# Last block before each normalisation: the second token half's product as two products of 256 columns

## The chip, the core and the metric

The kernel runs on one core of one Trainium2 chip. The metric is the device time of one execution in microseconds. Every profile shown is of one execution, taken by the hardware profiler.

## The reference

A trunk of two decoder layers over 256 tokens of width 2048, float32. Each layer is a token mixer and a gated ConvFFN (inner width 5632), and each sub-layer ends in a residual sum and a LayerNorm:

```python
for layer in range(DEPTH):
    if layer % N_MIXERS == 0:
        mixed = hgrn2_mixer(h, hg_w_in[occ], hg_norm_g[occ], hg_w_out[occ], lower_bounds[layer])
    else:
        mixed = chunked_gmlp(h, sg_w_in[occ], ..., sg_w_out[occ])
    h = layer_norm(ALPHA * h + mixed, ln1_g[layer], ln1_b[layer])
    ffn = conv_ffn(h, ffn_w_up[layer], ...)
    h = layer_norm(ALPHA * h + ffn, ln2_g[layer], ln2_b[layer])
```

`layer_norm` needs the mean and the variance of a whole row of 2048 values before any of it can be scaled. There are four such norms, one behind each sub-layer.

## The kernel before

**Data.** The 256 tokens are two halves of 128, `t` = 0 and 1. `z` (128 x 2 x 2048) holds the residual stream by tokens. `X` and `Y` hold activations turned, feature on the partition, as a rounded part `hi` and a rest `lo`; a product is three matmuls (hi by hi, hi by lo, lo by hi). Weights come as chunks of 4 x 128 rows by 512 columns (`CK`, `NB`): one DMA on the SP queue into `raw` (`fetch`, L80, 3 buffers), a cast to `whi` on ScalarE (L97) and a subtraction to `wlo` on VectorE (L98), each in two pieces. There are 3 buffers of `whi` and `wlo`, and one extra in the pool `xp`, so that four chunks can be held at a joint. `chunk` takes the next chunk and keeps three on the way (`ahead`).

**Products.** `block_a` makes tokens by features: for each column block of 512 it accumulates over the chunks into one PSUM tile for each token half (L127 to L129), then calls `evac`. With `staggered`, which is set for the last column block (`c == 3`) before a norm, the chunks are held and half 0 is finished and evacuated before half 1 begins (L144 to L149). `block_b` makes features by tokens (L163, L170); with `halves`, in the first FFN block behind a norm, all products that need only half 0 of the tokens come before those that need half 1 (L183 to L186). The first block of the gMLP input does the same with three chunks in `block_a`. The HGRN output uses `staggered_pass` (L664 to L679): one chunk for each of the four column blocks, half 0 through all four, then half 1.

**Joint.** `add_z` gives the evacuation: VectorE adds PSUM into `z` (L398, L400) and, in the last pass, takes `bn_stats` over the 512 columns (L402); after block 3 of a token half `after` runs: `bn_aggr` (L335), a square root on ScalarE (L336), a reciprocal (L337), four rescales of `z` (L371), and `turn`: four times four transposes on TensorE (L308) into a PSUM tile `pt` (2 buffers), scale and bias by three ScalarE activations (L315) and one VectorE row (L317) into `turn` (2 buffers), then a cast into `X` on ScalarE and a subtraction into `X` on VectorE (both L320). Behind the last norm two VectorE rows apply scale and bias (L365, L368) and `z` is stored. `tc.high_priority()` wraps these evacuations. A scheduler sets the order of rows on each engine when the program is built; on the chip each engine runs its rows in that order.

The norms stand behind `hgrn_out` (joint 1), `ffn(0)` (joint 2), `gmlp` (joint 3) and `ffn(1)` (the end).

Of the kernel before, what the change touches and what calls it, by code (L numbers as in the profile page):

```python
# [8 lines left out]
F32 = mybir.dt.float32  # L9
# [6 lines left out]
P = 128  # L16
# [7 lines left out]
LN_EPS = 1e-5  # L24
RMS_EPS = 1e-6
NB = 512
CK = 4
HEADS = 16
LEVELS = (1, 4, 16)
# [11 lines left out]
class Trunk:  # L41
# [72 lines left out]
    def block_a(self, act, ka, w, k0, nch, c0, evac, staggered=False, halves=False):  # L114

        nc = self.nc
        ps = [self.acc.tile([P, NB], F32, tag="acc", name="pa") for _ in range(2)]
        n = [0, 0]

        def part(ch, ci, t):  # L120
            hi, lo = ch
            for kk in range(CK):
                k = ka + ci * CK + kk
                xh = act[:, k, 0, t * P : (t + 1) * P]
                xl = act[:, k, 1, t * P : (t + 1) * P]
                last = n[t] == nch * CK - 1
                nc.tensor.matmul(ps[t], xh, hi[:, kk, :], start=n[t] == 0, stop=False)  # L127
                nc.tensor.matmul(ps[t], xh, lo[:, kk, :], start=False, stop=False)  # L128
                nc.tensor.matmul(ps[t], xl, hi[:, kk, :], start=False, stop=last)  # L129
                n[t] += 1  # L130

        take = lambda ci: self.chunk(w, k0 + ci * CK, c0)
        first = max(0, nch - 4) if staggered else nch
        head = []
        if halves:
            head = [take(ci) for ci in range(min(3, nch))]
            for t in range(2):
                for ci, ch in enumerate(head):
                    part(ch, ci, t)
        for ci in range(len(head), first):  # L140
            ch = take(ci)
            for t in range(2):
                part(ch, ci, t)
        held = [take(ci) for ci in range(first, nch)]  # L144
        for t in range(2):
            for i, ch in enumerate(held):
                part(ch, first + i, t)
            if held:
                evac(t, ps[t])  # L149
        if not held:  # L150
            for t in range(2):
                evac(t, ps[t])

    def block_b(self, act, w, nch, c0, evac, halves=False):

# [184 lines left out]
    def norm(self, name, l, store=None):  # L340


        nc = self.nc
        g, b = self.a[name + "_g"][l], self.a[name + "_b"][l]
        self.ln = ExitStack()
        self.lnp = self.ln.enter_context(
            self.tc.tile_pool(name=f"{name}{l}", bufs=1, side="right")
        )
        self.xps = ExitStack()
        self.xp = self.xps.enter_context(  # L350
            self.tc.tile_pool(name=f"x{name}{l}", bufs=1, side="right")
        )
        self.stats = [
            self.small.tile([P, 4, 6], F32, tag=f"stats{t}", name="stats") for t in range(2)
        ]
        self.gbc = [self.broadcast(self.lnp, g, c, f"g{c}") for c in range(4)]
        self.bbc = [self.broadcast(self.lnp, b, c, f"b{c}") for c in range(4)]

        def after(t):
            mv = self.mean_rstd(self.stats[t])  # L360
            mean, rstd = mv[:, 0:1], mv[:, 1:2]
            for c in range(4):
                zz = self.z[:, t, c * NB : (c + 1) * NB]
                if store:
                    nc.vector.scalar_tensor_tensor(  # L365
                        zz, zz, mean, self.gbc[c], ALU.subtract, ALU.mult
                    )
                    nc.vector.scalar_tensor_tensor(zz, zz, rstd, self.bbc[c], ALU.mult, ALU.add)  # L368
                    store(t, c)
                else:  # L370
                    nc.vector.tensor_scalar(zz, zz, mean, rstd, ALU.subtract, ALU.mult)  # L371
                    self.turn(t, 4 * c, g=(name + "_g", l), b=(name + "_b", l))

        self.after_stats = after
# [11 lines left out]
    def add_z(self, c, first=False, last=False):  # L386


        nc = self.nc

        def evac(t, ps):
            with self.tc.high_priority() if last else nullcontext():
                step(t, ps)

        def step(t, ps):
            zz = self.z[:, t, c * NB : (c + 1) * NB]
            if first:
                nc.vector.scalar_tensor_tensor(zz, zz, ALPHA, ps, ALU.mult, ALU.add)  # L398
            else:
                nc.vector.tensor_tensor(zz, zz, ps, ALU.add)  # L400
            if last:
                nc.vector.bn_stats(self.stats[t][:, c, :], zz)  # L402
                if c == 3:
                    self.after_stats(t)

        return evac
# [257 lines left out]
    def staggered_pass(self, act, ka, w, k0):  # L664

        nc = self.nc
        ev = [self.add_z(c, last=True) for c in range(4)]
        held = [self.chunk(w, k0, c * NB) for c in range(4)]
        for t in range(2):
            for c in range(4):  # L670
                hi, lo = held[c]
                ps = self.acc.tile([P, NB], F32, tag="acc", name="pa")
                for kk in range(CK):
# [229 lines left out]
```

## Time and profile before

| | |
|---|---|
| median of 3 runs | 2241.09 us (2240.43 to 2241.46) |
| the profiled execution's own time | 2240.33 us |
| its span | 2238.6 us |
| TensorE busy | 2216.0 us, 99% |
| VectorE busy | 1470.8 us, 66% |
| ScalarE busy | 1106.0 us, 49% |
| DMA | 430.14 MB, 192 GB/s on average |

Shares are over the whole span. In the stretch around a joint they differ: from 1505 to 1515 us TensorE is busy for 8.84 of 10 us and VectorE for all 10. Times in rows are from the start of the span. A row of the timeline gives start, duration, engine, line and shape, and in brackets the idle time ahead of it with what ended it. A row's duration reaches past the start of the next row on the same engine where they are pipelined, so the time a row takes of its queue is read from start to start.

### The profile page before, as it was taken

The page shows a single profiled execution, that of the slowest core. Times are in us where ns is not written, and L with a number is a line of the kernel's source. Part 1 is how long each engine was busy: PE and PEld are TensorE (multiplying, and loading weights), DVE is VectorE, ACT ScalarE, POOL GpSimd, SP SyncE. Part 2 cuts the span into 40 slices and gives each one's busy share as a digit, 9 for nine tenths or more (in the row PEclk, how much of TensorE's full clock was granted, in tenths as well). Part 3 has the DMA queues.
Part 4 walks back from the last instruction along what each step waited for, and adds up shares of the span by engine and source line. Part 5 has one row for each costly group of instructions (what it writes and reads, how often), then busy time and mean ns, then how long its engine had stood idle before and what let it go on. Part 6 is the DMA issues. An engine that isn't in the chain of part 4 may idle for free.

```text
span 2238.6 us, 31751 instructions
## 1 busy us (share of the span) xinstructions
PE 2216.0 (99%) x12781; PEld 1910.7 (85%) x12781; DVE 1470.8 (66%) x2327; ACT 1106.0 (49%) x1698; POOL 48.4 (2%) x102
## 2 busy tenths in 40 slices
PE   8999999999999999999999999999999999999998
PEld 7888888889888888888888888888888888888886
DVE  5877677667675666456666676566765666466755
ACT  5666565646443554344444545455544444344542
POOL 4000000000000000000000000000000000000000
PEclk9999999999999999999999999999999999999999
DMA  7454645555566555555555675655565655555563
GB/s 262 157 180 144 204 151 170 207 169 191 204 222 197 198 192 189 197 198 188 191 199 177 211 224 185 231 182 188 188 230 184 207 189 196 198 188 191 185 207 113
DMA packets 214052, 430.14 MB, mean 192 GB/s; under 512 B 7544, under 2 KB 8336, under 8 KB 213904
## 3 DMA queue, kind: packets, MB, share of 16 engines
q1 hardware_dynamic: 209536, 415.26, 55.5%
q0 software_dynamic: 4368, 12.85, 1.9%
q8 instruction: 100, 1.64, 0.3%
q14 instruction: 48, 0.39, 0.0%
HBM read 425.98 MB, written 2.10 MB: 191 GB/s over the span
## 4 chain that ended last, share of the span: by engine, by line
PE 94%; DVE 2%; ACT 1%; issue 1%; DMA 1%; SPq 0%; POOL 0%; DVEq 0%; POOLq 0%; ACTq 0%
PE pb L163 37%; PE pb L170 19%; PE pa L128 12%; PE pa L129 12%; PE pa L127 12%; DVE wlo L98 1%; PE pl L553 1%; PE pt L308 1%; ACT whi L97 1%; PE pg L755 0%; DMA bb<-in_sg_ln_b_dram 0%; PE pa L676 0%; PE pa L677 0%; PE pa L678 0%; DMA z<-in_x_dram 0%
## 5 line engine op out<-in xcount | busy, mean ns | idle before, releaser
L98 DVE TENSOR_TENSOR wlo<-raw,whi 128x1024 fp32r<-128x1024 f32 (+1 forms) x786 | 930.3, 1218 | 660.4 <-ACT whi L97 652.1
L163 PE MATMUL pb<-X,whi 128*128 128x512 f32 (+1 forms) x3960 | 1302.6, 384 | 1.9 <-DVE X L320 1.9
L97 ACT CAST whi<-raw 128x1024 fp32r<-128x1024 f32 (+1 forms) x786 | 790.1, 1047 | 859.3 <-PE pb L163 396.0
L170 PE MATMUL pb<-X,wlo 128*128 128x256 f32 x3840 | 1037.4, 278 | 0.0
L163 PEld LDWEIGHTS pb<-X,whi 128*128 128x128 f32 x3960 | 725.2, 188 | 143.5 <-DVE X L320 2.4
L170 PEld LDWEIGHTS pb<-X,wlo 128*128 128x128 f32 x3840 | 713.4, 188 | 5.9
L128 PE MATMUL pa<-wlo,Y 128*128 128x512 f32 x928 | 361.5, 390 | 0.0
L127 PE MATMUL pa<-whi,Y 128*128 128x512 f32 x928 | 361.4, 389 | 0.0
L129 PE MATMUL pa<-whi,Y 128*128 128x512 f32 x928 | 361.3, 389 | 0.0
L127 PEld LDWEIGHTS pa<-whi,Y 128*128 128x128 f32 x928 | 174.3, 188 | 36.0
L128 PEld LDWEIGHTS pa<-wlo,Y 128*128 128x128 f32 x928 | 174.3, 188 | 35.9
L129 PEld LDWEIGHTS pa<-whi,Y 128*128 128x128 f32 x928 | 174.3, 188 | 35.7
L208 ACT COPY rest<-pb 128x256 f32<-128x256 f32 x240 | 87.6, 368 | 100.9 <-PE pb L163 96.4
L128 PE MATMUL pa<-wlo,X 128*128 128x512 f32 x256 | 99.9, 390 | 0.0
L127 PE MATMUL pa<-whi,X 128*128 128x512 f32 x256 | 99.8, 390 | 0.0
L129 PE MATMUL pa<-whi,X 128*128 128x512 f32 x256 | 99.7, 389 | 0.0
L808 DVE SCALAR_TENSOR_TENSOR act<-a,cols,act 128x254 f32<-128x254 f32 (+1 forms) x176 | 73.1, 478 | 0.0
L128 PEld LDWEIGHTS pa<-wlo,X 128*128 128x128 f32 x256 | 48.1, 188 | 9.9
L129 PEld LDWEIGHTS pa<-whi,X 128*128 128x128 f32 x256 | 48.1, 188 | 9.8
L127 PEld LDWEIGHTS pa<-whi,X 128*128 128x128 f32 x256 | 48.1, 188 | 9.8
L400 DVE TENSOR_TENSOR z<-z,pa 128x512 f32<-128x512 f32 x40 | 27.3, 684 | 32.9 <-PE pa L129 29.0
L812 ACT ACTIVATE act<-act 128x256 f32<-128x256 f32 x88 | 33.8, 415 | 12.0 <-DVE act L808 11.8
(164 smaller groups left out, 1029.5 us busy)
## 6 DMA issues: line engine op xcount, KB each, us to landing
raw<-in_ffn_w_up_dram SPq DMA_DIRECT2D x176, 1024.0 KB, 4.9
raw<-in_ffn_w_down_dram SPq DMA_DIRECT2D x88, 1024.0 KB, 4.9
raw<-in_hg_w_in_dram SPq DMA_DIRECT2D x63, 1024.0 KB, 5.2
raw<-in_sg_w_in_dram SPq DMA_DIRECT2D x32, 1024.0 KB, 5.4
raw<-in_hg_w_out_dram SPq DMA_DIRECT2D x16, 1024.0 KB, 5.1
raw<-in_sg_w_out_dram SPq DMA_DIRECT2D x16, 1024.0 KB, 4.9
g<-in_ln_g_dram POOLq DMA_DIRECT2D x16, 256.0 KB, 6.4
b<-in_ln_b_dram POOLq DMA_DIRECT2D x16, 256.0 KB, 9.2
```

Of the source, the lines that this page charges most:

```text
L97: nc.scalar.copy(hi[:, s, :], raw[:, s, :])
L98: self.last_lo = nc.vector.tensor_tensor(lo[:, s, :], raw[:, s, :], hi[:, s, :].bitcast(F32), ALU.subtract)
L127: nc.tensor.matmul(ps[t], xh, hi[:, kk, :], start=n[t] == 0, stop=False)
L128: nc.tensor.matmul(ps[t], xh, lo[:, kk, :], start=False, stop=False)
L129: nc.tensor.matmul(ps[t], xl, hi[:, kk, :], start=False, stop=last)
L163: nc.tensor.matmul(ps[j][:, :, s], ch[0][:, k % CK, c], act[:, k, :, s], start=start and k == 0, stop=k == last, skip_group_check=halves,)
L170: nc.tensor.matmul(ps[j][:, 1, :], ch[1][:, k % CK, c], act[:, k, 0, :], start=False, stop=False, skip_group_check=halves,)
L208: nc.scalar.copy(r, ps[:, 1, :])
L308: nc.tensor.transpose(ps[:, j, :], self.z[:, t, k * P : (k + 1) * P], self.ident)
L400: nc.vector.tensor_tensor(zz, zz, ps, ALU.add)
L808: nc.vector.scalar_tensor_tensor(cv[:, d:], x[:, : S - d], self.c(("cw", l, 2 - d), f), cv[:, d:], ALU.mult, ALU.add,)
L812: nc.scalar.activation(cv, cv, AF.Silu)
```

## The change

In the last column block before each norm, half 1 of the tokens no longer fills one PSUM tile of 512 columns. A new function `in_halves` makes columns 0 to 255 over all chunks into one tile, evacuates it, then columns 256 to 511 into another. Half 0 is as before. `evac` and `step` take a slice; statistics of half 1 are kept as 8 records of 256 columns instead of 4 of 512, in all four blocks. For the blocks 0 to 2 of half 1 that means two `bn_stats` rows behind one add.

```diff
-        ps = [self.acc.tile([P, NB], F32, tag="acc", name="pa") for _ in range(2)]
+        ps = [self.acc.tile([P, NB], F32, tag="acc", name="pa") for _ in range(2 - staggered)]
...
-        first = max(0, nch - 4) if staggered else nch
+        first = 0 if staggered else nch
...
-        for t in range(2):
+        if held:
             for i, ch in enumerate(held):
-                part(ch, first + i, t)
-            if held:
-                evac(t, ps[t])
+                part(ch, first + i, 0)
+            evac(0, ps[0])
+            assert first == 0
+            pieces = [(ch, ka + i * CK + kk, kk) for i, ch in enumerate(held) for kk in range(CK)]
+            self.in_halves(act, pieces, lambda ps, s: evac(1, ps, s))
...
+    def in_halves(self, act, pieces, evac):
+        nc = self.nc
+        for h in range(2):
+            s = slice(h * HB, (h + 1) * HB)
+            ps = self.acc.tile([P, HB], F32, tag="acc", name="ph")
+            for n, ((hi, lo), k, kk) in enumerate(pieces):
+                xh, xl = act[:, k, 0, P:], act[:, k, 1, P:]
+                nc.tensor.matmul(ps, xh, hi[:, kk, s], start=n == 0, stop=False)
+                nc.tensor.matmul(ps, xh, lo[:, kk, s], start=False, stop=False)
+                nc.tensor.matmul(ps, xl, hi[:, kk, s], start=False, stop=n == len(pieces) - 1)
+            evac(ps, s)
...
-            self.small.tile([P, 4, 6], F32, tag=f"stats{t}", name="stats") for t in range(2)
+            self.small.tile([P, 4 * (1 + t), 6], F32, tag=f"stats{t}", name="stats")
+            for t in range(2)
...
             if last:
-                nc.vector.bn_stats(self.stats[t][:, c, :], zz)
-                if c == 3:
+                n = NB // (1 + t)
+                for i in range(s.start, s.stop, n):
+                    at = (c * NB + i) // n
+                    x = self.z[:, t, at * n : (at + 1) * n]
+                    nc.vector.bn_stats(self.stats[t][:, at, :], x)
+                if c == 3 and s.stop == NB:
                     self.after_stats(t)
...
+                if (t, c) == (1, 3):
+                    pieces = [(held[c], ka + kk, kk) for kk in range(CK)]
+                    self.in_halves(act, pieces, lambda ps, s: ev[3](1, ps, s))
+                    break
```

The scheduler also moves rows that the diff does not touch. Line numbers in the changed program are up to 26 higher: L334 is the turn's tensor-scalar (L317 before), L337 the subtraction into `X` (L320), L99 the weights' subtraction (L98), L352 the aggregate (L335), L354 the reciprocal (L337), L389 the rescale (L371), L416 and L418 the adds into `z` (L398, L400), L424 the statistics (L402), L325 the transposes (L308), L180 and L187 the products of `block_b` (L163, L170).

VectorE at joint 3, from the record of block 3, half 1, to the first subtraction into `X` of half 1. Before:

```order
L402 BN_STATS stats<-z 128x6
L98 TENSOR_TENSOR wlo<-raw,whi 128x1024
L335 BN_AGGR mv<-stats 128x2
L320 TENSOR_TENSOR X<-turn,X 128x4x128
L337 RECIPROCAL mv<-mv 128x1
L98 TENSOR_TENSOR wlo<-raw,whi 128x1024
L371 TENSOR_SCALAR z<-z,mv 128x512 x4
L98 TENSOR_TENSOR wlo<-raw,whi 128x1024
L317 TENSOR_SCALAR turn<-pt,cols 128x128
L98 TENSOR_TENSOR wlo<-raw,whi 128x1024
L320 TENSOR_TENSOR X<-turn,X 128x4x128
```

Now:

```order
L424 BN_STATS stats<-z 128x6
L99 TENSOR_TENSOR wlo<-raw,whi 128x1024
L352 BN_AGGR mv<-stats 128x2
L99 TENSOR_TENSOR wlo<-raw,whi 128x1024
L354 RECIPROCAL mv<-mv 128x1
L99 TENSOR_TENSOR wlo<-raw,whi 128x1024
L389 TENSOR_SCALAR z<-z,mv 128x512 x4
L99 TENSOR_TENSOR wlo<-raw,whi 128x1024 x2
L334 TENSOR_SCALAR turn<-pt,cols 128x128 x2
L99 TENSOR_TENSOR wlo<-raw,whi 128x1024
L337 TENSOR_TENSOR X<-turn,X 128x4x128 x2
```

One weights' subtraction more stands ahead of the rescale, and two subtractions and two tensor-scalars stand together ahead of the first `X`. Joint 2 has the same rows up to the rescale.

VectorE at joint 1, from the add of the last columns of half 1 to the rescale. Before:

```order
L400 TENSOR_TENSOR z<-z,pa 128x512
L317 TENSOR_SCALAR turn<-pt,cols 128x128
L402 BN_STATS stats<-z 128x6
L320 TENSOR_TENSOR X<-turn,X 128x4x128
L335 BN_AGGR mv<-stats 128x2
L98 TENSOR_TENSOR wlo<-raw,whi 128x1024
L337 RECIPROCAL mv<-mv 128x1
L320 TENSOR_TENSOR X<-turn,X 128x4x128
L371 TENSOR_SCALAR z<-z,mv 128x512 x4
```

Now:

```order
L418 TENSOR_TENSOR z<-z,ph 128x256
L334 TENSOR_SCALAR turn<-pt,cols 128x128
L424 BN_STATS stats<-z 128x6
L99 TENSOR_TENSOR wlo<-raw,whi 128x1024
L352 BN_AGGR mv<-stats 128x2
L337 TENSOR_TENSOR X<-turn,X 128x4x128
L334 TENSOR_SCALAR turn<-pt,cols 128x128
L99 TENSOR_TENSOR wlo<-raw,whi 128x1024
L354 RECIPROCAL mv<-mv 128x1
L337 TENSOR_TENSOR X<-turn,X 128x4x128
L389 TENSOR_SCALAR z<-z,mv 128x512 x4
```

Here too one weights' subtraction more comes ahead of the rescale.

TensorE at joint 3, the first FFN block with its products by token halves (60 for each half) and the transposes of half 1 in between. Before:

```order
L163 MATMUL pb<-X,whi 128x2x128 x47
L308 MATMUL pt<-ident,z 128x128 x8
L163 MATMUL pb<-X,whi 128x2x128 x13
L308 MATMUL pt<-ident,z 128x128 x4
L163 MATMUL pb<-X,whi 128x2x128 x4
L308 MATMUL pt<-ident,z 128x128 x4
L163 MATMUL pb<-X,whi 128x2x128 x56
L170 MATMUL pb<-X,wlo 128x256 x61
```

Now:

```order
L180 MATMUL pb<-X,whi 128x2x128 x48
L325 MATMUL pt<-ident,z 128x128 x8
L180 MATMUL pb<-X,whi 128x2x128 x12
L325 MATMUL pt<-ident,z 128x128 x8
L180 MATMUL pb<-X,whi 128x2x128 x60
L187 MATMUL pb<-X,wlo 128x256 x61
```

All sixteen transposes of half 1 now come ahead of the 60 products that read half 1.

## Rows read from the trace of the kernel before

**Rows 1.** The page: busy time, share and instructions of each engine; TensorE's granted clock in 40 slices, in tenths; the chain that ended last, by engine.

```profile
PE 2216.0 (99%) x12781; PEld 1910.7 (85%) x12781; DVE 1470.8 (66%) x2327; ACT 1106.0 (49%) x1698; POOL 48.4 (2%) x102
...
PEclk9999999999999999999999999999999999999999
...
PE 94%; DVE 2%; ACT 1%; issue 1%; DMA 1%; SPq 0%; POOL 0%; DVEq 0%; POOLq 0%; ACTq 0%
```

**Rows 2.** The timeline, TensorE at joint 1 and joint 3: the first products that read X of half 1, with the idle time ahead of them in brackets.

```profile
514.54 0.74 PE L163 MATMUL pb<-X,whi 128*128 128x256 f32 x4 [0.84 <-DVE X L320]
...
1514.98 0.73 PE L163 MATMUL pb<-X,whi 128*128 128x256 f32 x4 [1.08 <-DVE X L320]
```

**Rows 3.** The timeline, TensorE at the end: the first and the last of 54 products of 512 columns that follow each other.

```profile
2216.01 0.39 PE L127 MATMUL pa<-whi,Y 128*128 128x512 f32 x1
...
2228.03 0.39 PE L129 MATMUL pa<-whi,Y 128*128 128x512 f32 x1
```

**Rows 4.** The chain that ended last, at joint 3 (start, time, engine, line): products of 256 columns in a row.

```profile
1516.15 6.67 PE pb L163 x56
1522.82 7.32 PE pb L170 x61
```

**Rows 5.** Groups by line (busy us, mean ns of one | idle before): weight load, the add and the statistics of 512 columns, an add of 256 columns out of PSUM, the aggregate, the cast into X.

```profile
L170 PEld LDWEIGHTS pb<-X,wlo 128*128 128x128 f32 x3840 | 713.4, 188 | 5.9
...
L209 DVE TENSOR_TENSOR a<-pb,rest 128x256 f32<-128x256 f32 x88 | 33.0, 417 | 0.0
...
L400 DVE TENSOR_TENSOR z<-z,pa 128x512 f32<-128x512 f32 x40 | 27.3, 684 | 32.9 <-PE pa L129 29.0 <-PE pa L678 3.9
L402 DVE BATCH_NORM_STATS2 stats<-z 128x6 f32<-128x512 f32 x32 | 22.1, 692 | 0.7
...
L320 ACT CAST X<-turn 128x512 fp32r<-128x512 f32 x24 | 15.4, 641 | 0.0
...
L335 DVE BATCH_NORM_AGGREGATE mv<-stats 128x2 f32<-128x24 f32 x8 | 2.1, 260 | 0.2
```

**Rows 6.** The timeline, VectorE at joint 1: the add of block 2 of half 1, the first rescale, the first subtraction into X of half 1.

```profile
503.18 0.68 DVE L400 TENSOR_TENSOR z<-z,pa 128x512 f32<-128x512 f32 x1
...
509.38 1.91 DVE L371 TENSOR_SCALAR z<-z,mv 128x512 f32<-128x512 f32 x4
...
513.80 0.69 DVE L320 TENSOR_TENSOR X<-turn,X 128x512 fp32r<-128x512 f32 x1
```

**Rows 7.** The timeline, VectorE at joint 3: from the add of block 3 of half 1 to the first subtraction into X of half 1.

```profile
1505.25 0.69 DVE L398 SCALAR_TENSOR_TENSOR z<-z,pa 128x512 f32<-128x512 f32 x1
1505.86 0.41 DVE L317 TENSOR_SCALAR turn<-pt,cols 128x128 f32<-128x128 f32 x1
1506.18 0.68 DVE L402 BATCH_NORM_STATS2 stats<-z 128x6 f32<-128x512 f32 x1
1506.78 1.21 DVE L98 TENSOR_TENSOR wlo<-raw,whi 128x1024 fp32r<-128x1024 f32 x1
1507.90 0.26 DVE L335 BATCH_NORM_AGGREGATE mv<-stats 128x2 f32<-128x24 f32 x1
1508.08 0.63 DVE L320 TENSOR_TENSOR X<-turn,X 128x512 fp32r<-128x512 f32 x1
1508.62 0.15 DVE L337 RECIPROCAL mv<-mv 128x1 f32<-128x1 f32 x1
1508.69 1.21 DVE L98 TENSOR_TENSOR wlo<-raw,whi 128x1024 fp32r<-128x1024 f32 x1
1509.81 1.92 DVE L371 TENSOR_SCALAR z<-z,mv 128x512 f32<-128x512 f32 x4
1511.64 1.23 DVE L98 TENSOR_TENSOR wlo<-raw,whi 128x1024 fp32r<-128x1024 f32 x1
...
1514.23 0.69 DVE L320 TENSOR_TENSOR X<-turn,X 128x512 fp32r<-128x512 f32 x1
```

**Rows 8.** Joint 3: the timeline of ScalarE (the first cast for the next block) and of the SP queue (the transfer of its fourth chunk); and, of the tile raw from 1480 to 1520 us, the time from issue to landing.

```profile
1495.30 2.00 ACT L97 CAST whi<-raw 128x1024 fp32r<-128x1024 f32 x2 [0.72 <-PE pa L129]
...
1500.08 0.37 SPq L80 DMA_DIRECT2D raw<-in_ffn_w_up_dram  x1
...
DMA to landing us min/median/max: 4.8/5.0/6.3
```

**Rows 9.** The timeline at joint 2: VectorE's first rescale of half 1, its first subtraction into X, and TensorE's first product that reads it, with the transposes behind.

```profile
1234.44 1.91 DVE L371 TENSOR_SCALAR z<-z,mv 128x512 f32<-128x512 f32 x4
...
1238.39 0.69 DVE L320 TENSOR_TENSOR X<-turn,X 128x512 fp32r<-128x512 f32 x1 [0.79 <-ACT X L320]
...
1239.30 0.40 PE L127 MATMUL pa<-whi,X 128*128 128x512 f32 x1
1239.53 0.60 PE L308 MATMUL pt<-ident,z 128*128 128x128 f32 x4
```

**Rows 10.** The timeline, VectorE at the end, half 1: the add, the record, the aggregate and the first of the rows that scale and store.

```profile
2228.45 0.69 DVE L400 TENSOR_TENSOR z<-z,pa 128x512 f32<-128x512 f32 x1 [3.67 <-PE pa L129]
2229.18 0.69 DVE L402 BATCH_NORM_STATS2 stats<-z 128x6 f32<-128x512 f32 x1
2229.90 0.26 DVE L335 BATCH_NORM_AGGREGATE mv<-stats 128x2 f32<-128x24 f32 x1
2230.20 0.75 DVE L365 SCALAR_TENSOR_TENSOR z<-z,mv,g 128x512 f32<-128x512 f32 x1
```

More of the change, by code (lines that the diff above doesn't have):

```diff
@@ L26 @@
 NB = 512
+HB = NB // 2
 CK = 4
@@ L389, in add_z, with evac, step @@
         nc = self.nc
-        def evac(t, ps):
+        def evac(t, ps, s=slice(0, NB)):
             with self.tc.high_priority() if last else nullcontext():
-                step(t, ps)
-        def step(t, ps):
-            zz = self.z[:, t, c * NB : (c + 1) * NB]
+                step(t, ps, s)
+        def step(t, ps, s):
+            zz = self.z[:, t, c * NB + s.start : c * NB + s.stop]
             if first:
```

## The prediction, made before the change was run

> **What bounds the kernel now.** The share of busy time and the chain of waits come first: TensorE is busy for 99% of the span and holds 94% of the chain [rows 1]. Between the joints a matmul that becomes longer is paid for in full. So the question is local: what happens at the four joints where a normalised block ends. Joint 1 lies at about 480 to 523 us (HGRN output into the first FFN), joint 2 at 1204 to 1245 (FFN into gMLP), joint 3 at 1479 to 1523 (gMLP output into the second FFN), and the end at 2204 to 2238. At joints 1 and 3 the timeline of TensorE shows one wait each, 0.84 and 1.08 us, both for X written by VectorE in L320 [rows 2]: the second token half is turned too late. At joint 2 there is no such wait, since the first half of the gMLP input gives TensorE enough work. At the end everything after the last matmul is a chain on VectorE. So TensorE bounds joint 2, and the second half's chain of add, statistics, rescale and transpose bounds joints 1, 3 and the end.
>
> **TensorE's part of the change.** In the last block of a joint, 48 products of 512 columns become 96 of 256 (12 become 24 at joint 1). A product of 512 columns takes a slot of (2228.03 - 2216.01) / 53 = 0.2268 us [rows 3]. Products of 256 columns, each with its weight load, stand in the half-by-half FFN block: 56 in 6.67 us and 61 in 7.32 us, so 0.1191 and 0.1200 [rows 4]. I take 0.1195. That is 96 x 0.1195 - 48 x 0.2268 = 11.47 - 10.89 = +0.58 us at joints 2, 3 and the end, and a quarter of it, +0.15, at joint 1. Bounds: nothing (exactly half a slot), and 96 x 0.188 - 10.89 = +7.2 if the weight load's own 188 ns [rows 5] set the slot; the 61 products with a load each at 0.120 are nearest by far and exclude that end.
> The Trainium skill, page "TensorE: Matmul & The Clock Gate", section "Back-to-back issue gap", gives 262 cycles for 256 columns and 518 for 512. At the full clock that the rows show as granted [rows 1], 2.4 GHz, this would make a pair of halves only 2.5 ns dearer than the whole, +0.12 us per joint; the rows have 12 ns per pair, and the rows decide.
>
> **VectorE's part, at the end.** The chain from the last product to the mean is now add 0.73, statistics 0.72, then the aggregate [rows 10]. A half needs 417 ns for the add instead of 684, as L209 shows for 256 columns out of PSUM [rows 5]: -0.27. Statistics over 256 columns are not in the trace: 692 at most, 346 at least, and I take the same -0.27, because a 512-column statistic costs nearly what the 512-column add does. The aggregate reads 48 values instead of 24: +0.03 by the same slope. The first half's add and record hide under the second half's products. The end: +0.58 - 0.51 = **+0.1 us**.
>
> **VectorE's part at the joints.** The order of rows decides, because VectorE runs its rows as they stand and is full there. At joint 1 it goes without a gap from the add of block 2 at 503.18 to the first rescale at 509.38, 6.20 us [rows 6]. In the new order the same stretch has one weight conversion L98 more ahead of the rescale (it stood behind the last turn before), +1.13; every record of 512 becomes two of 256, +0.08 for each of four blocks, and the split add +0.07. Sum +1.5. From the rescale to the first L320 the rows are the same ones as before, so X comes 1.5 later, and TensorE, which already waits there, waits longer. **Joint 1: +1.5 us** (its +0.15 of products lies inside the wait).
>
> At joint 3 I replay the queue from starts of neighbours [rows 7]: add 0.61, turn's tensor-scalar 0.32, record 0.60, conversion 1.12, aggregate 0.18, X subtraction about 0.6, reciprocal 0.07. Before, add to rescale took 1509.81 - 1505.25 = 4.56. Now: half add 0.34, X 0.60, half record 0.34, conversion 1.12, aggregate 0.18, conversion 1.12, reciprocal 0.07, conversion 1.12 = 4.9, starting 0.58 later, and by my estimate 0.3 more because the conversion just ahead of the add is itself late. The rescale moves by 0.33 + 0.58 + 0.3 = 1.2. Behind it stood four rescales, a conversion, a tensor-scalar, a conversion, then the first X (1509.81 to 1514.23, 4.42 [rows 7]). Now stand four rescales, two conversions, two tensor-scalars, a conversion: 1.83 + 2.24 + 0.64 + 1.12 = 5.8. X comes 1.2 + 1.4 = 2.6 us later. TensorE gets 0.6 back, since the four transposes that split its last 60 products, 1514.98 to 1522.82 for 60 products that need 7.2 [rows 2, 4], are now done inside the wait. **Joint 3: +2.0 us.**
>
> Why the conversions crowd there: four weight chunks are held while the last block runs. Before, the second token half read chunk after chunk, so the first one came free after 12 of 48 products, and ScalarE's cast for the next block started at 1495.30 just when TensorE let it go [rows 8]. Two products in sequence read every chunk twice; the first one comes free after 60 of 96, some 5.5 us later. Casts, conversions and the next transfer all move behind the turn of the first half and into the second half's chain.
>
> At joint 2 the same VectorE rows put the rescale at about 1234.44 + 1.2 = 1235.65 [rows 9]; with 1.83 of rescales, one conversion, tensor-scalars and ScalarE's cast of 0.64 [rows 5] the first X ends at about 1240.4. Without any wait TensorE would reach the first product that needs it at 1239.30 + 0.58 + 0.36 (four transposes moved ahead of it) = 1240.2. The last transposes also wait for a buffer that the late tensor-scalars set free, which I put at 0.3 to 0.5. **Joint 2: +0.58 + 0.5 = +1.1 us.**
>
> **Sum.** 1.5 + 1.1 + 2.0 + 0.1 = +4.7 us. The profiled run took 2240.33 (span 2238.6), 0.76 under the median of the three timed runs; on that median the sum gives **2245.8 us**, 0.21% slower. A measurement of this kernel can tell about 0.2%, 4.5 us, from no change, so the forecast stands just beyond that line.
>
> **Rivals.**
> - *The shorter chain wins (not slower).* If VectorE gets through the moved conversions while TensorE still multiplies the second half, the rescale starts earlier by the 0.54 that the halves save, in joints 1 and 3. Then 0.15 - 0.54, 0.58, 0.58 - 0.54 and 0.1 make +0.3: 2241.4. It decides from the point where the rescale starts no later than at 509.38 and 1509.81. For it: the add and the record of the last block are plainly shorter. Against it: the order of rows, which puts conversions between them, and chunks that are free only after 60 of 96 products.
> - *A half costs exactly half.* Products of 256 at 0.1134 take the 0.58 and 0.15 away; the late X at joints 1 and 3 then still holds all but some 0.6 there, so about 4.7 - 1.8 = +2.9: 2244.0. The two rows at 0.119 and 0.120 speak against it. The Trainium skill's cycle table, in "TensorE: Matmul & The Clock Gate", section "Back-to-back issue gap", would make it nearly so.
> - *The late transfer shows (slower still).* The fourth chunk of the next block is fetched when the first is converted, at 1500.08 now and about 1506.2 then, and lands 4.8 to 6.3 us later [rows 8]. Its cast stands ahead of the turn's activations on ScalarE. At the slow end of that spread it adds 1.3 at joint 3. At joint 2 the products use the subtracted part at once, and three conversions there come, by the same replay, within about 0.2 us of their use, so each may hold TensorE for up to 0.6. Together +8: 2249.
> - *Faster.* All it could gain is both waits and the end, 0.84 + 1.08 + 0.51 = 2.4 us, 0.11%. More has no place in the trace.
>
> **Chances.** The forecast's case 0.72, from +3 to +7; the shorter chain 0.13, half for half 0.03, the late transfer 0.09, faster for a reason not seen 0.03. Of the forecast's 0.72 I put 0.45 beyond 4.5 us. Slower is 0.45 + 0.09 = 0.54, within 0.2% is 0.27 + 0.13 + 0.03 = 0.43, faster 0.03. The range goes from 2243.0 (+1.9: the forecast's case, half for half, and a margin below) to 2249.0 (+7.9: the late transfer nearly whole). It leaves out the shorter chain and faster, 0.16, and about 0.04 above.
>
> **What would show it.** Products of 256 at 0.119 to 0.121 us. At joint 1 TensorE's wait for X of 0.84 grows to about 2.3; at joint 3 that of 1.08 grows beyond 3, with transposes inside; at joint 2 a wait of some 0.5 appears. ScalarE's first cast of the next block starts 5 to 6 us later at joints 2 and 3, and the next transfer with it. The end gets 0.5 us shorter from the last product on. Wrong would be waits for X that shrink, half records that cost as much as whole ones, or a delay anywhere off the joints.

## The result, and the profile after

| | before | changed |
|---|---|---|
| median (8 runs each) | 2241.08 us | 2247.95 us |
| lowest to highest | 2240.2 to 2241.87 | 2246.16 to 2250.25 |
| ratio, 95% interval | | 1.003 (1.002 to 1.0039) |
| the profiled execution: time, span | 2240.33, 2238.6 | 2250.25, 2248.5 |

The change costs 6.9 us: slower by more than 0.2%, and inside the range of 2243.0 to 2249.0. The forecast of 2245.8 was 2.15 us too low. The profiled execution of the changed kernel is the longest of its eight, so its stretches are set below against further profiles. The medians of the experiments leave out two executions at a mean granted clock of 0.655 and 0.262, one of statistics only (3184.05 us) and one of the kernel before (8215.42 us).

The page after, answering to [rows 1] (busy time, share, instructions; then the granted clock in 40 slices):

```profile
PE 2219.9 (99%) x12937; PEld 1919.4 (85%) x12937; DVE 1473.4 (66%) x2347; ACT 1107.8 (49%) x1698; POOL 49.7 (2%) x102
...
PEclk9999999999999999999999999999999999999999
```

The page shows little: TensorE is busy for 3.9 us more, and no slice of the clock differs. The rest is in a few waits of 0.2 to 2 us. TensorE at joint 1 in the timeline (start, duration, in brackets the wait), answering to [rows 2]:

```profile
515.10 0.66 PE L325 MATMUL pt<-ident,z 128*128 128x128 f32 x4 [0.73 <-DVE turn L334]
516.84 0.80 PE L180 MATMUL pb<-X,whi 128*128 128x256 f32 x4 [1.08 <-DVE X L337]
517.43 1.06 PE L325 MATMUL pt<-ident,z 128*128 128x128 f32 x4
518.14 8.03 PE L180 MATMUL pb<-X,whi 128*128 128x256 f32 x56
```

The wait of 0.84 has become two, 1.81 together. And the last row is a surprise: 56 products took 8.03 us, where [rows 4] has 6.67. The reason is in the windows (stretch, its length, TensorE busy with its count, granted clock, DMA share, GB/s):

```profile
514.00:516.00 2.00, 1.03 (x8) 1.00 0.71 273
516.00:518.00 2.00, 1.17 (x7) 0.84 0.31 60
518.00:520.00 2.00, 2.00 (x12) 0.50 0.98 359
520.00:522.00 2.00, 2.00 (x15) 0.81 0.57 134
522.00:524.00 2.00, 2.00 (x19) 1.00 0.96 348
```

Behind the two waits the granted clock fell from 1.00 to 0.50, from 2.4 to 1.2 GHz, for some 3 us. In the kernel before it stays at 1.00 at this place.

Joint 2, answering to [rows 9]: TensorE, with two waits for the weights' lower part that before does not have, and the first product that reads X of half 1, for which it does not wait; then VectorE's rescale and its first two subtractions into X of half 1:

```profile
1237.56 0.50 PE L129 MATMUL pa<-wlo,X 128*128 128x512 f32 x1 [0.27 <-DVE wlo L99]
...
1243.07 0.50 PE L129 MATMUL pa<-wlo,X 128*128 128x512 f32 x1 [0.23 <-DVE wlo L99]
...
1245.20 0.40 PE L128 MATMUL pa<-whi,X 128*128 128x512 f32 x1
```

```profile
1239.97 1.91 DVE L389 TENSOR_SCALAR z<-z,mv 128x512 f32<-128x512 f32 x4
...
1244.05 1.29 DVE L337 TENSOR_TENSOR X<-turn,X 128x512 fp32r<-128x512 f32 x2
```

Joint 3, where everything now lies 6.95 us later (z of half 0 is added at 1499.49; 1492.54 before). ScalarE's casts for the next block and the SP queue's transfer of its fourth chunk, answering to [rows 8]; then VectorE from the second half add on, answering to [rows 7]; then TensorE, answering to [rows 2]:

```profile
1508.86 1.06 ACT L98 CAST whi<-raw 128x1024 fp32r<-128x1024 f32 x1
...
1518.69 2.00 ACT L98 CAST whi<-raw 128x1024 fp32r<-128x1024 f32 x2 [1.75 <-DMA raw<-in_ffn_w_up_dram]
```

```profile
1513.72 4.12 SPq L81 DMA_DIRECT2D raw<-in_ffn_w_up_dram  x2
```

```profile
1512.46 1.23 DVE L99 TENSOR_TENSOR wlo<-raw,whi 128x1024 fp32r<-128x1024 f32 x1 [0.36 <-ACT whi L98]
1513.61 0.41 DVE L416 SCALAR_TENSOR_TENSOR z<-z,ph 128x256 f32<-128x256 f32 x1
...
1514.88 1.21 DVE L99 TENSOR_TENSOR wlo<-raw,whi 128x1024 fp32r<-128x1024 f32 x1
1516.00 0.37 DVE L352 BATCH_NORM_AGGREGATE mv<-stats 128x2 f32<-128x48 f32 x1
1516.28 1.16 DVE L99 TENSOR_TENSOR wlo<-raw,whi 128x1024 fp32r<-128x1024 f32 x1
1517.36 0.15 DVE L354 RECIPROCAL mv<-mv 128x1 f32<-128x1 f32 x1
1517.43 1.20 DVE L99 TENSOR_TENSOR wlo<-raw,whi 128x1024 fp32r<-128x1024 f32 x1
1518.55 1.91 DVE L389 TENSOR_SCALAR z<-z,mv 128x512 f32<-128x512 f32 x4
...
1524.41 1.29 DVE L337 TENSOR_TENSOR X<-turn,X 128x512 fp32r<-128x512 f32 x2
```

```profile
1512.61 0.28 PE L168 MATMUL ph<-whi,Y 128*128 128x256 f32 x1
...
1519.15 1.11 PE L325 MATMUL pt<-ident,z 128*128 128x128 f32 x8 [0.82 <-DVE z L389]
...
1523.11 1.09 PE L325 MATMUL pt<-ident,z 128*128 128x128 f32 x8 [1.44 <-DVE turn L334]
1525.16 7.33 PE L180 MATMUL pb<-X,whi 128*128 128x256 f32 x60 [0.96 <-DVE X L337]
```

Read against the 6.95: the first cast is another 6.6 us later, the fourth transfer 6.7, the rescale 1.8, the first X 3.2. Three conversions stand between the statistics and the rescale, where there were two, and TensorE waits three times, 3.22 us together instead of 1.08.

The end, VectorE, answering to [rows 10]:

```profile
2238.76 0.42 DVE L418 TENSOR_TENSOR z<-z,ph 128x256 f32<-128x256 f32 x1 [3.64 <-PE ph L168]
2239.21 0.43 DVE L424 BATCH_NORM_STATS2 stats<-z 128x6 f32<-128x256 f32 x1
2239.67 0.37 DVE L352 BATCH_NORM_AGGREGATE mv<-stats 128x2 f32<-128x48 f32 x1
2240.08 0.75 DVE L383 SCALAR_TENSOR_TENSOR z<-z,mv,g 128x512 f32<-128x512 f32 x1
```

From the add to the first row that scales it takes 1.32 us, 1.75 before: the shorter chain is real, and the dearer products take it back.

### The profile page after: what moved, and what is told of

It is laid out like the page before. It is cut to its first block, busy times and chain, and to the rows that moved or that the text cites. A ratio compares the mean times of both kernels' runs of the same rounds, so it can differ in the third digit from the quotient of the medians.

```text
span 2248.5 us, 32084 instructions
## 1 busy us (share of the span) xinstructions
PE 2219.9 (99%) x12937; PEld 1919.4 (85%) x12937; DVE 1473.4 (66%) x2347; ACT 1107.8 (49%) x1698; POOL 49.7 (2%) x102
## 3 DMA queue, kind: packets, MB, share of 16 engines
q8 instruction: 101, 1.65, 0.3%
## 4 chain that ended last, share of the span: by engine, by line
PE 92%; DVE 3%; ACT 2%; issue 2%; DMA 1%; SPq 0%; POOL 0%; DVEq 0%; POOLq 0%; ACTq 0%
PE pb L180 36%; PE pb L187 19%; PE pa L129 11%; PE pa L130 11%; PE pa L128 11%; DVE wlo L99 1%; ACT whi L98 1%; DMA z<-in_x_dram 1%; PE pl L575 1%; ACT turn L332 0%; DMA bb<-in_sg_ln_b_dram 0%; PE pg L781 0%; PE ph L167 0%; PE ph L166 0%; PE ph L168 0%
## 5 line engine op out<-in xcount | busy, mean ns | idle before, releaser
L99 DVE TENSOR_TENSOR wlo<-raw,whi 128x1024 fp32r<-128x1024 f32 (+1 forms) x786 | 930.5, 1219 | 663.8 <-ACT whi L98 653.9
L180 PE MATMUL pb<-X,whi 128*128 128x512 f32 (+1 forms) x3960 | 1303.4, 384 | 2.1 <-DVE X L337 2.0
L98 ACT CAST whi<-raw 128x1024 fp32r<-128x1024 f32 (+1 forms) x786 | 790.2, 1047 | 859.4 <-PE pb L180 399.2
L187 PE MATMUL pb<-X,wlo 128*128 128x256 f32 x3840 | 1037.3, 278 | 0.0
L180 PEld LDWEIGHTS pb<-X,whi 128*128 128x128 f32 x3960 | 725.6, 188 | 143.7 <-DVE X L337 2.9
L187 PEld LDWEIGHTS pb<-X,wlo 128*128 128x128 f32 x3840 | 713.1, 188 | 5.9
L128 PE MATMUL pa<-whi,Y 128*128 128x512 f32 x880 | 342.5, 389 | 0.0
L130 PE MATMUL pa<-whi,Y 128*128 128x512 f32 x880 | 342.5, 389 | 0.0
L129 PE MATMUL pa<-wlo,Y 128*128 128x512 f32 x880 | 342.4, 389 | 0.0
L129 PEld LDWEIGHTS pa<-wlo,Y 128*128 128x128 f32 x880 | 165.2, 188 | 34.3
L128 PEld LDWEIGHTS pa<-whi,Y 128*128 128x128 f32 x880 | 165.3, 188 | 34.1
L130 PEld LDWEIGHTS pa<-whi,Y 128*128 128x128 f32 x880 | 165.3, 188 | 33.9
L418 DVE TENSOR_TENSOR z<-z,pa 128x512 f32<-128x512 f32 x37 | 25.3, 684 | 29.3 <-PE pa L130 25.3
```

Source lines behind the costliest of these rows:

```text
L98: nc.scalar.copy(hi[:, s, :], raw[:, s, :])
L99: self.last_lo = nc.vector.tensor_tensor(lo[:, s, :], raw[:, s, :], hi[:, s, :].bitcast(F32), ALU.subtract)
L180: nc.tensor.matmul(ps[j][:, :, s], ch[0][:, k % CK, c], act[:, k, :, s], start=start and k == 0, stop=k == last, skip_group_check=halves,)
L187: nc.tensor.matmul(ps[j][:, 1, :], ch[1][:, k % CK, c], act[:, k, 0, :], start=False, stop=False, skip_group_check=halves,)
```

## The experiments

Theory A: at joints 2 and 3 the loss comes from weight chunks held longer, so that casts and conversions come late and stand ahead of half 1's rescale; at joint 1 from the order of rows. Theory B: the finer statistics. Theory C: the dearer products. Theory D: the clock behind a wait. Theory E came later and concerns a stretch off the joints.

The program can be cut at marks that every kernel has: z of half 0 added in the last block of a joint; the first product with the weights' lower part of the next FFN block (behind joints 1 and 3); the first transpose of the gMLP's own weights, `pw`, at 1296.92. Each column is such a stretch of the profile, one profile for each kernel, in us, less the same stretch before (30.11, 79.76, 195.62, 30.11 and 21.03 us; "gMLP" runs from `pw` to z at joint 3). Left out are what lies ahead of joint 1 (-0.3 to +0.9) and the two stretches from joint 1 to 2 and from 3 to the end (-0.4 to +0.8 each, changed joint or not).

| kernel | joint 1 | joint 2 | gMLP | joint 3 | end | median less before's |
|---|---|---|---|---|---|---|
| changed | 2.75 | 1.67 | 1.53 | 2.73 | 0.22 | +6.9 |
| statistics only | 0.37 | -0.01 | -0.59 | 0.21 | 0.17 | +0.2 |
| joint 1 only | 1.24 | 0.03 | 0.52 | -0.12 | 0.04 | +2.1 |
| all but joint 1 | -0.01 | 1.69 | 1.22 | 2.73 | 0.28 | +6.1 |
| by chunk | 1.18 | 0.57 | 0.53 | -0.62 | 0.22 | +2.4 |
| joint 1, gated | 0.44 | -0.03 | 1.67 | 0.04 | 0.03 | +0.7 |
| joint 1, long wait | 9.30 | 0.00 | 3.14 | 0.04 | 0.03 | +11.4 |
| joint 3 by chunk | 0.00 | -0.02 | 0.17 | -0.63 | 0.00 | -0.4 |
| joint 2 only | 0.00 | 1.66 | 4.00 | -0.07 | 0.08 | +2.5 |
| joint 3 only | 0.00 | 0.02 | -0.61 | 2.73 | 0.06 | +3.0 |
| changed, 3 rows | 2.66 | 1.65 | 1.53 | 2.73 | 0.31 | +8.8 |
| before, 3 rows | 0.00 | 0.02 | 0.84 | 0.00 | -0.01 | +0.7 |
| joint 3 by chunk, 3 rows | -0.07 | -0.02 | 0.71 | -0.62 | 0.02 | 0.0 |

A joint repeats within 0.1 us from kernel to kernel, while a median has an interval of 2 us on either side. So the verdicts rest on the columns.

At joint 1 the mark hides 0.23 us. TensorE's products of L163 from 515 us to the mark, by shape, in the kernel before, and the same products (L180 there) from 516.4 us in joint 1 only (busy us, mean ns of one):

```profile
...
L163 PE MATMUL pb<-X,whi 128*128 128x512 f32 x1 | 0.4, 396 | 0.0
```

```profile
L180 PE MATMUL pb<-X,whi 128*128 128x256 f32 x59 | 7.4, 282 | 0.0
```

Where joint 1 is as before, and in the gated kernel, one product of 512 columns, a slot of 0.23, stands ahead of the mark; in statistics only there are two; in the other kernels that change joint 1 there is none, and it follows behind the mark. The stretch from joint 1 to 2 agrees: without statistics only and the gated kernel it is 0.0 or 0.6 longer than before where joint 1 is as before, and 0.2 or 0.8 where it is changed. So a changed joint 1 costs 1.4 to 1.5 where the column says 1.2, and the records alone cost 0.1 there and not 0.37.

**Statistics only.** Half 1 keeps one product of 512 columns, at joint 1 too.

```diff
-            self.in_halves(act, pieces, lambda ps, s: evac(1, ps, s))
+            for i, ch in enumerate(held):
+                part(ch, first + i, 1)
+            evac(1, ps[1])
```

> Half 1 is one product of 512 columns again at every joint; only its statistics are kept as 8 records of 256. Theory A (the chunks held longer cost the time at joints 2 and 3, the order of VectorE's rows at joint 1): +0.3 to +0.8 us on the kernel before, 2241.4 to 2241.9, since one record more per block costs about 0.08 us of VectorE and the conversions stay where they were; the first cast of the next block at joint 3 stays at about 1495. Theory B (the finer statistics load VectorE at the joints, where it is full): at least half of the +6.9 us, 2244.5 or more. Theory C (the dearer products): no more than 0.3.

Measured 2241.78, ratio 1.0001 (0.9992 to 1.001). Theory B falls: the records cost 0.1 to 0.2 us at joints 1, 3 and the end.

**Joint 1 only, and all but joint 1.** The two products stay in `staggered_pass` alone, or in `block_a` alone; the records go with them. For the second:

```diff
-                if (t, c) == (1, 3):
-                    pieces = [(held[c], ka + kk, kk) for kk in range(CK)]
-                    self.in_halves(act, pieces, lambda ps, s: ev[3](1, ps, s))
-                    break
```

> Only joint 1 is changed; joints 2, 3 and the end are as before. Theory A: VectorE's rows at joint 1 stand as in the changed kernel, so the rescale and the first X of half 1 come 1.5 us later against the stretch's start and TensorE waits for it; +1.5 us if the granted clock stays at 1.00 there, +2.7 if it falls again as in the profile of the changed kernel: 2242.6 to 2243.8. Theory C (the dearer products): 24 products for 12, +0.2 us, 2241.3. If the clock falls in one execution and not in another, the runs spread over about 1 us more than those of the kernel before.

> Joint 1 is as before; joints 2, 3 and the end are as in the changed kernel. Theory A: about +1.5 at joint 2, +2.5 at joint 3, +0.2 at the end, so +4.2 us, 2245.3; with the one part at joint 1 the two make up the whole +6.9. Theory C (the dearer products): 0.58 at joints 2, 3 and the end, +1.7, 2242.8. If the +1.6 us between 1300 and 1345 us in the profile of the changed kernel was chance, the stretch from the end of joint 2 to joint 3 is as long here as before.

Measured 2243.73, 1.0011 (1.0002 to 1.002), and 2247.66, 1.0032 (1.0021 to 1.0044). Joint 1 alone costs 1.24 by the column and 1.5 with the mark's 0.23, with the clock at 1.00 throughout; that is Theory A's lower figure. Its first product of half 1 comes 1.49 us later against z of half 0, which is added at 492.23 (492.35 before):

```profile
515.91 0.73 PE L180 MATMUL pb<-X,whi 128*128 128x256 f32 x4 [1.08 <-DVE X L337]
516.49 0.60 PE L325 MATMUL pt<-ident,z 128*128 128x128 f32 x4
516.84 6.90 PE L180 MATMUL pb<-X,whi 128*128 128x256 f32 x56
```

The runs spread over 4.0 us, those of the kernel before over 5.0, so the spread says nothing of the clock. Without joint 1 the losses at joints 2 and 3 are those of the changed kernel to 0.02 us, 4.4 us together where Theory C gives 1.2. The stretch behind joint 2 was not as long as before but 1.2 us longer; it is taken up below.

**By chunk.** The same products and records, in another order:

```diff
-        for h in range(2):
...
-            for n, ((hi, lo), k, kk) in enumerate(pieces):
+        for i in range(0, len(pieces), CK):
+            for h, ps in enumerate(tiles):
...
+                for n, ((hi, lo), k, kk) in list(enumerate(pieces))[i : i + CK]:
```

> Same products of 256 columns and same records as the changed kernel, but both column halves go through the four chunks side by side: chunk 0 for both halves, then chunk 1, and so on, so that a chunk comes free after 24 of 96 products and not after 60. Theory A (held chunks): joints 2 and 3 lose nearly all of their loss, +0.6 at joint 2 for the products, -0.3 to +0.5 at joint 3, +0.1 at the end, joint 1 as in the changed kernel (+1.5 to +2.7): +2 to +4 us, 2243 to 2245; the first cast of the next block at joint 3 goes back by 5.5 to 6.5 us against z of half 0. Theory C (the dearer products themselves, or the finer statistics): nothing changes, +6.9 us, 2248.

Measured 2243.96, 1.0012 (1.0003 to 1.0021), an interval that only touches that of all but joint 1. Joint 2 falls from 1.67 to 0.57, which is the price of the products, and joint 3 from +2.73 to -0.62, below the -0.3 to +0.5 expected. ScalarE's cast and TensorE at joint 3 in this kernel (z of half 0 is added at 1496.56):

```profile
1499.48 2.00 ACT L98 CAST whi<-raw 128x1024 fp32r<-128x1024 f32 x2 [0.87 <-PE ph L170]
```

```profile
1514.26 1.12 PE L328 MATMUL pt<-ident,z 128*128 128x128 f32 x8 [0.19 <-DVE z L392]
```

The first cast comes 2.92 us behind z, as before (2.76), and not 9.37. The waits of 0.82, 1.44 and 0.96 are one of 0.19. Between the last record and the rescale VectorE again has two conversions, and the rescale stands 17.10 us behind z (17.27 before, 19.06 in the changed kernel). The products and records are the same; with their order two things changed, the moment at which a chunk is let go and that of the first half's add, which now comes only 1.07 us ahead of the second's. That add and its record take some 0.7 of VectorE's queue, against 3.35 us between the two kernels at joint 3. So the held chunks are the cause at joint 3, and at joint 2 of all but the price of the products. Theory C is left with 0.57 at joint 2.

**Joint 1, gated.** Joint 1 only; the cast of the next block's fourth chunk is queued behind half 1's square root, its subtraction behind the rescale.

```diff
-            self.convert(*self.fetch())
+            with self.tc.issue_after(self.root.ins), self.tc.issue_after(self.scaled.ins):
+                self.convert(*args)
```

> As the run with only joint 1 changed, but the cast and the subtraction of the fourth chunk of the first FFN block are put behind the square root and the rescale of half 1 (on ScalarE and VectorE). Ahead of the rescale VectorE then has one conversion between the add of the last columns and the rescale, as in the kernel before, and ScalarE's square root no longer stands behind a cast that waits for its transfer. Theory A (the order of rows at joint 1): rescale 1.3 to 1.8 us earlier than in the run with only joint 1 changed, at 509 to 509.5, first product of half 1 at 514.6 to 515.3 and not 515.9; joint 1 costs +0.1 to +0.7 against before and not +1.2: 2241.3 to 2242.3. Theory C (products and records of 256 themselves cost the time): rescale and products of half 1 stay where they were, +2 us, 2243.7.

Measured 2241.69, 1.0003 (0.9994 to 1.0012). VectorE from the aggregate on:

```profile
507.86 0.36 DVE L358 BATCH_NORM_AGGREGATE mv<-stats 128x2 f32<-128x48 f32 x1
508.14 0.63 DVE L343 TENSOR_TENSOR X<-turn,X 128x512 fp32r<-128x512 f32 x1
508.68 0.15 DVE L362 RECIPROCAL mv<-mv 128x1 f32<-128x1 f32 x1
508.75 0.39 DVE L340 TENSOR_SCALAR turn<-pt,cols 128x128 f32<-128x128 f32 x1
509.06 1.91 DVE L399 TENSOR_SCALAR z<-z,mv 128x512 f32<-128x512 f32 x4
```

The rescale stands at 509.06, against 510.76 in joint 1 only and 509.38 before [rows 6], and joint 1 costs 0.44 and not the 1.5 of joint 1 only, with one wait of 1.08 in place of two. The order of rows is the cause there. What it gains on the rescale it loses to an X of half 0 and a second tensor-scalar that moved behind it: the first product of half 1 comes at 515.42, just outside the 514.6 to 515.3 expected.

**Joint 1, long wait.** Joint 1 only, with the aggregate of half 1 taken nine times.

```diff
-        nc.vector.bn_aggr(mv, stats)
+        for _ in range(1 + 8 * more):
+            nc.vector.bn_aggr(mv, stats)
```

> As the run with only joint 1 changed, with the aggregate of half 1 at joint 1 taken nine times one after another, so that TensorE's wait there becomes some 4 us longer (three more conversions get ahead of the rescale as well). Question: does the wait bring down TensorE's granted clock, as at joint 1 in the profile of the changed kernel? Theory D (the clock falls behind such a wait, surely when it is longer): the granted clock reads 0.50 in some 2 us behind the wait, the 60 products of half 1 take 8 us or more and not 6.8, and the time is 1.2 to 1.5 us above what the wait alone gives: about 2243.7 + 4 + 1.4 = 2249. Rival (the fall there had another cause): the clock stays at 1.00 and the time is 2247.5 to 2248.

Measured 2252.4, 1.0053 (1.0041 to 1.0066). The waits grew more than I had reckoned, to 1.91, 3.76, 1.30 and 0.37. Windows at joint 1:

```profile
518.00:520.00 2.00, 1.07 (x8) 1.00 1.03 376
520.00:522.00 2.00, 0.70 (x4) 0.55 1.01 394
522.00:524.00 2.00, 1.63 (x8) 0.50 0.04 14
524.00:526.00 2.00, 2.00 (x12) 0.50 0.00 0
526.00:528.00 2.00, 2.00 (x15) 0.74 0.00 0
```

The clock falls behind the wait of 3.76 and comes back while products run, so Theory D holds for a long wait. Behind the changed kernel's own two waits at joint 1 (0.72 or 0.73, then 1.07 or 1.08) four profiles were taken: the clock fell in two (changed; changed, 3 rows) and stayed in two (joint 1 only; by chunk). A fall costs 1.4 to 1.6 us: 2.66 and 2.75 against 1.18 and 1.24. What decides between them stays open.

**Joint 2 only, joint 3 only.** All other joints have one product of 512 columns.

```diff
+            if not two:
+                for i, ch in enumerate(held):
+                    part(ch, first + i, 1)
+                evac(1, ps[1])
+                return
```

> Only joint 2 is changed, as in the changed kernel (two products in sequence). Theory A: local loss at joint 2 as in the profiles of the changed kernel and of the run without joint 1, +1.7 us between z of half 0 and the products behind the joint (0.6 for the products, the rest from casts and conversions that come late, with two waits of TensorE of about 0.25 us for the weights' lower part): 2242.7. The prediction's +1.1 would give 2242.1. Theory D for the rest of the loss: the granted clock stays at 1.00 behind these short waits, so the runs spread no more than those of before.

> Only joint 3 is changed, as in the changed kernel (two products in sequence). Theory A: first cast of the next block 6 to 7 us later against z of half 0, first product of half 1 about 3 us later, +2.7 us: 2243.7. Theory D: if the waits of 0.8, 1.4 and 1.0 us there bring the granted clock down in some executions, those are 1 to 2 us longer than the rest, at a lower mean clock (0.997 and not 0.999), and the median is 2244 to 2245.5.

Measured 2243.37, 1.0011 (1.0002 to 1.002), and 2243.86, 1.0014 (1.0004 to 1.0023). Both losses stand alone as they stood together. At joint 3 the profile shows no fall, nor do the three others with the same three waits there (0.8, 1.4 and 1.0 us). Joint 2's profile has one, but 110 us behind the joint, in the gMLP, where TensorE waited 2.83 us for y:

```profile
1346.00:1348.00 2.00, 0.00 (x0) 1.00 0.00 0
1348.00:1350.00 2.00, 1.93 (x10) 0.63 0.89 209
1350.00:1352.00 2.00, 2.00 (x8) 0.51 0.82 320
```

VectorE there stands behind a row of gains, `gb`, that is fetched when a buffer comes free (in before, then in this kernel):

```profile
1333.88 0.75 DVE L745 SCALAR_TENSOR_TENSOR v<-v,mv,gb 128x512 f32<-128x512 f32 x1 [0.71 <-DMA gb<-in_sg_ln_g_dram]
```

```profile
1336.96 0.75 DVE L772 SCALAR_TENSOR_TENSOR v<-v,mv,gb 128x512 f32<-128x512 f32 x1 [2.57 <-DMA gb<-in_sg_ln_g_dram]
```

Theory E: this wait makes up the rest, since by the columns the joints sum to 5.8 of the 6.9 us (6.1 with the mark's 0.23).

**Three rows.** `gb` and `bb` get three buffers instead of two, in the changed kernel and in the one before.

```diff
-                gb = self.broadcast(g2, a["sg_ln_g"][0], c, "gb")
+                gb = self.broadcast(g2, a["sg_ln_g"][0], c, "gb", bufs=3)
```

> The changed kernel with three buffers instead of two for the broadcast rows gb and bb of the gMLP block, so that VectorE there does not wait for a transfer that a freed buffer starts (in the profiles TensorE's wait for y at 1344 to 1351 us goes from 0 to 2.8 us with no change ahead of it). Theory E (this wait, and the clock that falls behind it, make up what the joints leave open: the four joints give 1.2 + 1.7 + 2.7 + 0.2 = 5.8 of the measured 6.9): that wait is gone, 2246.5 (5.4 above the kernel before), runs spread less than 3 us. Rival (the open 1.1 us lies at the joints): no change, 2248.

> The kernel before with the same three buffers for gb and bb. Theory E: the wait for y of 0.4 us in the profile of before is gone, -0.4 us, 2240.7, and the changed kernel with three buffers stands 5.8 us above this one. Rival: it stands 6.9 above it.

Measured 2249.38, 1.0038 (1.0025 to 1.0051), and 2241.29, 1.0003 (0.9994 to 1.0012). Theory E's remedy fails: TensorE's wait for y is 1.64 and 0.92 us with three buffers (1.94 and 0.40 with two), and the distance is 8.1 us. The third buffer did not take the wait away, so it says little on what the wait costs. The profiles themselves say more. In all fourteen the gMLP column is, to 0.6 us, that wait less the 0.40 of before, and 1.6 more in the two profiles where the clock fell behind it: joint 2 only (wait of 2.83, column 4.00) and the long wait (1.97, column 3.14). Behind waits of 2.14 (joint 1, gated) and 1.94 (changed) it did not fall.

**The parts that gained.** Joint 3 alone by chunk (the two edits above together, `two` set for the gMLP output only), then with three rows.

> Only joint 3 is changed, and there by chunk (both column halves through the four chunks side by side); joints 1, 2 and the end are the kernel before's. Theory A: the first product of half 1 at joint 3 does not wait for X, the stretch from z of half 0 to the products with the lower weights is 29.5 us and not 30.1, as in the run with all joints by chunk: -0.6 us, 2241.0, less than the runs can tell from no change. Theory C: +2.7 us, as at joint 3 in the changed kernel, 2244.3.

> The kernel before with joint 3 alone by chunk and three buffers for gb and bb: the parts that gained. -0.6 at joint 3 and -0.4 at the wait for y: 2240.1, 1.0 us under the kernel before, still within what a measurement can tell from no change.

Measured 2240.65, 0.9999 (0.999 to 1.0008), and 2240.64, 1.0 (0.9991 to 1.0009). The 0.6 us at joint 3 is there in three profiles (by chunk, and these two), and is less than the runs can tell from no change.

## Why the prediction came out as it did

- **TensorE's part: right.** A product of 256 columns takes 0.120 us (seven of them from 1511.77 to 1512.61), so the +0.58 stands; joint 2 by chunk, where hardly anything else is left, has 0.57. The rival of a half for exactly half is out. The Trainium skill's 262 cycles in "TensorE: Matmul & The Clock Gate", section "Back-to-back issue gap", would be, as an estimate, 0.109 us at 2.4 GHz; the trace differs, and decides.
- **The end: right.** +0.1 forecast; 0.2 to 0.3 measured. A half record takes 0.33 of the queue, about half a whole one's 0.60; the aggregate of 48 values takes 0.36 instead of 0.26, where I had +0.03.
- **Joint 1: right, but for the clock.** The forecast has the rescale and the first X 1.5 later by the order of rows. From the add of block 2 to the rescale it is 7.63 us instead of 6.20, and the first product of half 1 comes 1.5 later. Four transposes split the last 60 products in both kernels, so joint 1 gets no credit for them. TensorE's wait of 0.84 became 1.81 and not the 2.3 that were named. Gating one chunk gives about 1.0 back. The step that was missing is the granted clock, +1.5 in two of four profiles.
- **Joint 3: the mechanism right, the sum too small.** 2.7 against 2.0. The forecast's reason, chunks free only after 60 of 96 products, is what the order by chunk takes away. The mis-sized term is the "0.3 more" for the conversion ahead of the last half's add, and ahead of it the "5.5 us later" for the first chunk, whose cast comes 6.6 later. The add starts at 1513.61, some 0.7 us behind the end of the last product (1512.61 and 0.28), because that conversion itself waited 0.36 for its cast. With the add 1.4 us later than before against z, and not 0.9, the rescale comes 1.8 later and not 1.2. The replay behind it held: add to rescale 4.94 us, 4.9 forecast.
- **Joint 2: the late rows right, the wait wrong.** 1.7 against 1.1. The rescale is late here as at joint 3. But the forecast's 0.5 was a wait for X of half 1 and for a transpose buffer, and neither shows: the first product that reads X comes at 1245.20, some 0.5 us behind X. TensorE waited for the weights' lower part instead, 0.27 and 0.23 us, which the prediction had only in its rival of the late transfer; that they sum to 0.5 is luck. From start to start the products around these waits take 1.0 us more than their slots; with 0.57 for the products that is 1.6 of the 1.67.
- **The rivals.** The shorter chain would have won with the chunks let go early: at joint 3 by chunk it does, -0.6. Of the late transfer both parts showed: at joint 2 two conversions held TensorE, and at joint 3 ScalarE waited 1.75 us for the transfer, but VectorE's order held X longer.
- **The total: too small.** Of the 2.2 us that the forecast lacks, joints 2 and 3 make 1.3 and the end 0.1. The joints sum to 1.5 + 1.7 + 2.7 + 0.2 = 6.1 of 6.9 us. The other 0.8 is off the joints or in the clock, where the prediction has no term; a delay off the joints was among its signs of being wrong, and the gMLP stretch of the changed kernel has one, 1.5 us.
- **What stays open.** The clock at joint 1 adds 1.5 at times, and what decides it no run shows. The gMLP stretch is 1.2 to 4.0 us longer in the four profiles with joint 2 in sequence (one of them with three rows), and -0.6 to +3.1 in those seven with joint 2 as before and two rows, before itself among them. It follows the wait for y; whether a late joint 2 makes that wait longer, or chance does, the runs don't settle.

## What to carry to other kernels

Splitting a product to shorten the chain behind it also decides how long its operands are held: walk the pieces through each weight chunk side by side, so that a chunk is let go as early as before. At a joint where one engine runs its rows without a gap, count what the new order puts ahead of the critical row; one conversion of 1.1 us more outweighs the 0.5 us that halves save. A change of a few us in 2240 is read from stretches between fixed marks, which repeat to about 0.1 us, rather than from medians; but look whether the same rows stand ahead of the mark, since one product moved past it was worth 0.23 here.

## What the runs showed of the hardware

The granted clock fell to 0.50 behind two waits of 0.73 and 1.08 us with eight transposes and a few products around them, in two of four profiles with the same waits; it came back some 3 us later, and a fall cost 1.4 to 1.6 us. In the gMLP, where a broadcast row landed late, it fell behind waits of 2.83 and 1.97 us and not behind 2.14 and 1.94; behind three waits of 0.8, 1.4 and 1.0 us at joint 3 it fell in none of four profiles. So a wait of TensorE can cost more than its length, and the length alone does not tell when.
